# RMS norms of a two-layer decoder trunk: ScalarE takes the logarithm of the mean straight from PSUM, and VectorE makes the mean for Newton's step from the same PSUM tile

## The chip, the core and the metric

The kernel runs on one core of a Trainium2 chip. A core has five engines that each work through a program of their own, in order: TensorE (PE; its weight loads are shown as PEld), VectorE (DVE), ScalarE (ACT), GpSimd (POOL) and SyncE (SP), which here issues nearly all DMAs. They wait for one another through semaphores. The metric is device time in microseconds for one execution, as the median of several.

## What is computed

A decoder trunk of two layers over 1024 tokens of width 1024: an mLSTM layer with an MLP, a shared low-rank key/value latent, then a latent attention layer with an MLP. What matters here is the norm, which stands in front of and behind every block:

```python
def rmsnorm(x, g):
    xf = x.astype(jnp.float32)
    y = xf * lax.rsqrt(jnp.mean(xf * xf, axis=-1, keepdims=True) + EPS)
    return (y * g.astype(jnp.float32)).astype(x.dtype)

x = x + g1[:, None, :] * rmsnorm(y, norm_g[l, 1])
h = modulate(rmsnorm(x, norm_g[l, 2]), sh2, sc2)
y = sqrelu_mlp(h, mlp_w1[l], mlp_w2[l])
x = x + g2[:, None, :] * rmsnorm(y, norm_g[l, 3])
```

The latents of the attention layer (`c_kv`, 256 wide, and `cq`, 384 wide) are normed in the same way.

## The kernel before

**Layout.** Activations are held transposed: features on the 128 partitions, tokens along the free dimension, in two halves of 512 tokens. A tensor of width 1024 is eight tiles of 128x512. Each projection is done in three matrix products on values split into a high and a low part (L280, L281, L282). VectorE and ScalarE split the weights (`wsplit`: ScalarE L238 copies the high part, VectorE L239 subtracts) and the activations (`split_mod`: ScalarE L499, VectorE L500), and they empty PSUM.

**The norm.** `square_to` squares the tiles on ScalarE (L482) and adds them on VectorE (L486). `sums_rstd` (L488) multiplies the sum with a matrix of ones on TensorE (L490), so that every partition of a PSUM tile `pc` (128x512) holds the sum over the features of each token. VectorE reads that tile and makes the mean plus epsilon, `v` (L492). `rsqrt_` then takes the logarithm of `v` on ScalarE (L455), the exponential of minus half of it (L456), which is a first value `y` of the reciprocal root, and improves it on VectorE by a step of Newton's method in three instructions (L457, L458, L459): square of `y`, times `v` times -0.5, plus 1.5 times `y`. `sums_rstd` runs 16 times in the program, each time on 128x512. `rsqrt_` is also called 18 times on 128x4 tiles from other places (L535, L861 feed it), which the change leaves as they are.

**Who uses it.** `residual` (L939) multiplies the output of a block by the result (L950) and adds the old stream to it (L953); for the second attention half the old stream comes back by DMA into `tmc` tiles (`x_cols`, L920), and the new one goes out by DMA (L956). `post` and `post_second` norm the new stream and multiply it (L509). `latent` norms the key/value latent and the query latent (`cq`: L1690, applied on VectorE at L1706 and split by L499 and L500).

**What runs beside it.** The dense MLP of one token half runs beside the mixer of the other (`two_streams`). In it `hid` adds two PSUM tiles into kept ones: L1083 and L1084 read one `ps` tile, of which there are two, and `squares` (L980, L981 on ScalarE) squares the result. L1209 and L1211 load weights and copy them.

**What sets the order.** The program is recorded in Python in one order. The tile framework then schedules it with its own timing simulation, so each engine's order is its outcome, with `high_priority` and `issue_after` as hints. After that each engine keeps its order strictly. The framework also adds the waits: after a writer, before a buffer is reused, and between engines that read the same PSUM tile. The `tmc` tiles come from a ring of six, the `pc` and `ps` tiles from two each.

Of the kernel before, what the change touches and what calls it, by code (L numbers as in the profile page):

```python
# [9 lines left out]
F32 = mybir.dt.float32  # L10
# [3 lines left out]
AF = mybir.ActivationFunctionType  # L14
# [3 lines left out]
P = 128  # L18
# [6 lines left out]
EPS = 1e-6  # L25
# [57 lines left out]
def kernel(  # L83
# [27 lines left out]
    nc = tc.nc  # L111
# [26 lines left out]
    def tmc(dt=F32):  # L138
        return sb.tile([P, 512], dt, tag="tmc", bufs=TMC, name=f"tmc_{next(uid)}")
# [10 lines left out]
    def pc():  # L150
        return pp.tile([P, 512], F32, tag="pc", bufs=2, name=f"pc_{next(uid)}")
# [7 lines left out]
    def const(shape, dt, name):  # L159
        return sb.tile(shape, dt, tag=name, bufs=1, name=name)  # L160
# [287 lines left out]
    mcol = const([NH, 9], F32, "mcol")  # L448
    nc.vector.memset(mcol, 0.0)
    Cst = const([P, 4, VE], F32, "Cst")  # L450


    def rsqrt_(y, v, t):

        nc.scalar.activation(t, v, AF.Ln)  # L455
        nc.scalar.activation(y, t, AF.Exp, scale=-0.5)  # L456
        nc.vector.tensor_mul(t, y, y)  # L457
        nc.vector.scalar_tensor_tensor(t, t, -0.5, v, ALU.mult, ALU.mult)  # L458
        nc.vector.scalar_tensor_tensor(y, t, 1.5, y, ALU.add, ALU.mult)  # L459
# [12 lines left out]
    def rstd_steps(blocks, n):  # L472

        accs = []
        for b in blocks:
            square_to(accs, b)
        yield
        return sums_rstd(accs[0], n, tmc())
# [9 lines left out]
    def sums_rstd(acc, n, y):  # L488
        pt = pc()
        nc.tensor.matmul(pt, ones, acc, start=True, stop=True)  # L490
        v, t = tmc(), acc
        nc.vector.tensor_scalar(v, pt, 1.0 / n, EPS, ALU.mult, ALU.add)  # L492
        rsqrt_(y, v, t)
        return y

    def split_mod(hi, lo, u, sh):
# [37 lines left out]
    def rms_rows(v):  # L534
        nc.vector.tensor_scalar(v, v, 1.0 / D, EPS, ALU.mult, ALU.add)  # L535
        y, w = small(4), small(4)
        rsqrt_(y, v, w)
        return y
# [271 lines left out]
    def chunks0(hf):  # L810
# [4 lines left out]
        for j in range(4):  # L815
# [31 lines left out]
            for q, nv in enumerate(nvs):  # L847

                d, y, ss = small(4), small(4), small(4)
                sq = tmc()  # L850
                nc.scalar.activation(
                    sq.rearrange("p (b i e) -> p b i e", b=2, i=2), nv[:, :, :, 0:128], AF.Square
                )
                den = nv[:, :, :, 128]
                nc.vector.tensor_scalar(m4(y), den, -1.0, None, ALU.mult)
                nc.vector.tensor_max(m4(d), den, m4(y))
                enm = hf.gc[:, j, 16 + 4 * q : 20 + 4 * q].rearrange("p (i b) -> p b i", b=2)
                nc.vector.tensor_max(m4(d), m4(d), enm)
                nc.vector.scalar_tensor_tensor(d, d, EPS, d, ALU.mult, ALU.mult)
                nc.vector.reduce_sum(ss, sq.rearrange("p (a e) -> p a e", e=P), axis=AX.X)  # L860
                nc.vector.scalar_tensor_tensor(d, ss, 1.0 / P, d, ALU.mult, ALU.add)  # L861
                rsqrt_(y, d, ss)
                t1 = tmc()
                nc.vector.tensor_mul(
                    t1.rearrange("p (b i e) -> p b i e", b=2, i=2), nv[:, :, :, 0:128],
                    m4(y).unsqueeze(3).to_broadcast([P, 2, 2, P]),
                )
                t1s.append(t1)
# [736 lines left out]
    def latent(hf, behind):  # L1605
# [47 lines left out]
        def scaled(o, m):  # L1653

            pt = proj(m)
            if m < 2:

                evac(o, pt)
                pt = o

            if not rx:
                rx.append(sums_rstd(hf.xx, D, Cst.rearrange("p a b -> p (a b)")[:, :H]))
            nc.vector.tensor_mul(o, pt, rx[0])
            return o
# [1273 lines left out]
```

## Time and profile before

| | us |
|---|---|
| median of 3 runs (lowest, highest) | 2321.11 (2319.03, 2321.47) |
| the profiled execution's own time | 2317.84 |
| its span, first to last instruction | 2316.1 |
| TensorE busy, weight loads busy | 2276.3, 1918.0 |
| VectorE, ScalarE, GpSimd busy | 1698.5, 1126.6, 84.1 |
| mean granted TensorE clock | 0.997 |

A profile shows one execution. "Busy" counts time in which an engine had an instruction running; matrix products overlap, so a busy TensorE may still be slowed. A list of waits gives, for each engine and line, how long it stood idle and which engine's instruction released it. A timeline prints each instruction's start, duration, engine, line, operation and tiles, and in brackets the idle time before it and who ended it.

### The profile page before, as it was taken

Reading aid. Unit: us, or ns where it says so; the run is one execution under the profiler, and the core shown is the slowest. Engines: PE = TensorE matmul, PEld = TensorE weight load, DVE = VectorE, ACT = ScalarE, POOL = GpSimd, SP = SyncE. Lnnn points to the kernel's source line nnn. Section 1 sums busy time; section 2 is a strip of 40 time slices with the busy share of each in tenths; the row PEclk is TensorE's granted clock in tenths of the full one; section 3 lists DMA queues with packets and bytes.
Section 4 is the critical chain, followed back from the end, with each engine's and each line's share of the span. In section 5 each row is a group of like instructions: output and inputs, shape, how many; then the busy total and the mean of one; then the engine's idle time right before and its main releaser. Section 6 shows DMA issues by size and latency. Waiting matters only on the chain.

```text
span 2316.1 us, 32512 instructions
## 1 busy us (share of the span) xinstructions
PE 2276.3 (98%) x12010; PEld 1918.0 (83%) x12010; DVE 1698.5 (73%) x2782; ACT 1126.6 (49%) x1919; POOL 84.1 (4%) x164
## 2 busy tenths in 40 slices
PE   8999999999999999999999999999999999999998
PEld 6888788888887878778888788888888888989997
DVE  6676777889887877777765687666666388788776
ACT  4365435765334445545444555433444354555453
POOL 1000000001122210000000000000000000000000
PEclk9999999999999999999999999999999999999999
DMA  9543464668999887656775654764324352445432
GB/s 314 180 129 112 135 182 154 196 221 266 329 282 295 284 293 259 195 187 204 242 253 192 225 197 151 254 230 157 129 95 157 107 168 82 153 144 176 125 110 110
DMA packets 401647, 444.36 MB, mean 192 GB/s; under 512 B 27123, under 2 KB 289328, under 8 KB 401488
## 3 DMA queue, kind: packets, MB, share of 16 engines
q1 hardware_dynamic: 388544, 397.09, 53.6%
q0 software_dynamic: 12944, 45.20, 5.3%
q8 instruction: 94, 1.54, 0.3%
q14 instruction: 65, 0.53, 0.1%
HBM read 343.65 MB, written 98.57 MB: 191 GB/s over the span
## 4 chain that ended last, share of the span: by engine, by line
PE 75%; DMA 9%; DVE 9%; issue 4%; ACT 2%; POOL 0%; SPq 0%; DVEq 0%; ACTq 0%; POOLq 0%
PE ps L280 13%; PE ps L282 13%; PE ps L281 13%; PE pm L280 8%; PE pm L281 8%; PE pm L282 8%; DMA raw<-in_mlp_w_dram 4%; PE pc L281 2%; PE pc L280 2%; PE pc L282 2%; DMA raw<-s 1%; DVE wl L239 1%; DVE k L247 1%; PE pc L1988 1%; DVE sm L1791 1%
## 5 line engine op out<-in xcount | busy, mean ns | idle before, releaser
L238 ACT CAST wh<-raw 128x1024 fp32r<-128x1024 f32 (+2 forms) x317 | 321.4, 1016 | 437.2 <-PE ps L281 177.4
L239 DVE TENSOR_TENSOR wl<-raw,wh 128x1024 fp32r<-128x1024 f32 (+2 forms) x317 | 375.3, 1186 | 202.6 <-ACT wh L238 169.9
L280 PE MATMUL ps<-k,wh 128*128 128x512 f32 (+1 forms) x1252 | 476.0, 380 | 4.8 <-DVE tmc L1084 1.4
L282 PE MATMUL ps<-k,wl 128*128 128x512 f32 (+1 forms) x1252 | 468.4, 374 | 0.5 <-DVE wl L239 0.5
L281 PE MATMUL ps<-k,wh 128*128 128x512 f32 (+1 forms) x1252 | 467.9, 374 | 0.0
L280 PEld LDWEIGHTS ps<-k,wh 128*128 128x128 f32 x1252 | 236.2, 189 | 51.9 <-issue 2.8
L282 PEld LDWEIGHTS ps<-k,wl 128*128 128x128 f32 x1252 | 236.0, 189 | 43.4 <-DVE wl L239 1.0
L281 PEld LDWEIGHTS ps<-k,wh 128*128 128x128 f32 x1252 | 236.3, 189 | 41.4 <-issue 1.4
L247 DVE TENSOR_TENSOR k<-k,pm 128x512 f32<-128x512 f32 (+1 forms) x250 | 192.5, 801 | 63.3 <-PE pm L282 62.8
L280 PE MATMUL pm<-wh,hd 128*128 128x512 f32 x488 | 193.5, 396 | 3.5 <-ACT raw L1793 2.3
L282 PE MATMUL pm<-wh,hd 128*128 128x512 f32 x488 | 190.5, 390 | 0.0
L281 PE MATMUL pm<-wl,hd 128*128 128x512 f32 x488 | 190.3, 390 | 0.0
L280 PEld LDWEIGHTS pm<-wh,hd 128*128 128x128 f32 x488 | 91.7, 188 | 25.3 <-ACT raw L1793 4.6
L282 PEld LDWEIGHTS pm<-wh,hd 128*128 128x128 f32 x488 | 91.6, 188 | 19.9 <-DVE hd L500 0.5
L281 PEld LDWEIGHTS pm<-wl,hd 128*128 128x128 f32 x488 | 91.8, 188 | 18.4 <-issue 0.5
L390 DVE SCALAR_TENSOR_TENSOR tma<-raw,cond,tma 128x512 f32<-128x512 f32 x120 | 89.6, 747 | 16.6 <-DMA raw<-in_ada_w_dram 7.8
L281 PE MATMUL pm<-hd,wk 128*128 128x512 f32 x256 | 100.0, 391 | 1.7 <-DVE hd L500 1.7
L1793 ACT ACTIVATE raw<-pm,sm 128x128 f32<-128x128 f32 (+3 forms) x64 | 47.6, 743 | 111.0 <-DVE sm L1792 106.4
L280 PE MATMUL pm<-hd,wk 128*128 128x512 f32 x256 | 100.9, 394 | 0.6 <-ACT hd L499 0.6
L280 PE MATMUL pm<-hd,wh 128*128 128x512 f32 x256 | 99.2, 389 | 1.1 <-ACT hd L499 1.1
L282 PE MATMUL pm<-hd,wl 128*128 128x512 f32 x256 | 99.8, 390 | 0.1
L281 PE MATMUL pm<-hd,wh 128*128 128x512 f32 x256 | 99.6, 390 | 0.2 <-DVE hd L500 0.2
(497 smaller groups left out, 4828.1 us busy)
## 6 DMA issues: line engine op xcount, KB each, us to landing
raw<-in_mlp_w_dram SPq DMA_DIRECT2D x176, 512.0 KB, 4.5
raw<-in_ada_w_dram SPq DMA_DIRECT2D x64, 512.0 KB, 4.6
raw<-in_mlp_w_dram SPq DMA_DIRECT2D x128, 256.0 KB, 4.7
raw<-in_a_w_in_dram SPq DMA_DIRECT2D x44, 512.0 KB, 4.5
lo<-wl POOLq DMA_DIRECT2D x32, 512.0 KB, 6.1
wk<-lo SPq DMA_DIRECT2D x64, 256.0 KB, 4.4
xs<-k SPq DMA_DIRECT2D x40, 256.0 KB, 4.7
raw<-in_a_w_out_dram SPq DMA_DIRECT2D x16, 512.0 KB, 4.9
```

Source lines behind the costliest of these rows:

```text
L238: nc.scalar.copy(hi[:, :n], r[:, :n])
L239: i = nc.vector.tensor_sub(lo[:, :n], r[:, :n], hi[:, :n].bitcast(F32))
L247: return f(*a, **k)
L280: nc.tensor.matmul(o, lh, rh, start=start, stop=False)
L281: nc.tensor.matmul(o, lh, rl, start=False, stop=False)
L282: pe_last[0] = nc.tensor.matmul(o, ll, rh, start=False, stop=stop)
L390: nc.vector.scalar_tensor_tensor(acc, r[kk], cond[:, k : k + 1], acc, ALU.mult, ALU.add)
L1791: nc.vector.reduce_max(m, f, axis=AX.X, negate=True)
L1793: nc.scalar.activation(pr[:, :n], f, AF.Exp, bias=m, scale=SCALE, accum_out=l)
L1988: nc.tensor.transpose(pt[:, ts(m, P)], u.prs[i][:, ts(kb, P)], ident)
```

## The change

`sums_rstd` no longer calls `rsqrt_`. ScalarE takes the logarithm straight from the PSUM tile, with the scale 1/n as an immediate and epsilon from a new constant tile `epsc` as the bias; the exponential follows; VectorE then makes the mean `v` from the same PSUM tile, and `newton` holds the three instructions that stood at the end of `rsqrt_`. The other callers of `rsqrt_` execute what they did.

```diff
+    epsc = const([P, 1], F32, "epsc")
+    nc.vector.memset(epsc, EPS)
 
     def rsqrt_(y, v, t):
 
         nc.scalar.activation(t, v, AF.Ln)
         nc.scalar.activation(y, t, AF.Exp, scale=-0.5)
+        newton(y, v, t)
+
+    def newton(y, v, t):
+
         nc.vector.tensor_mul(t, y, y)
         nc.vector.scalar_tensor_tensor(t, t, -0.5, v, ALU.mult, ALU.mult)
         nc.vector.scalar_tensor_tensor(y, t, 1.5, y, ALU.add, ALU.mult)
...
         pt = pc()
         nc.tensor.matmul(pt, ones, acc, start=True, stop=True)
         v, t = tmc(), acc
+        nc.scalar.activation(t, pt, AF.Ln, bias=epsc, scale=1.0 / n)
+        nc.scalar.activation(y, t, AF.Exp, scale=-0.5)
         nc.vector.tensor_scalar(v, pt, 1.0 / n, EPS, ALU.mult, ALU.add)
-        rsqrt_(y, v, t)
+        newton(y, v, t)
         return y
```

In the changed program later lines have moved down: the logarithm is L498, the exponential L499, the mean L500, Newton's step L463 to L465, and lines from there on are 6 to 8 higher than before. The numbers behind tile names are 2 higher.

The scheduler moves other instructions around the 16 norms. Three places matter for the prediction.

The first is the norm of the query latent of the first half (`cq`), on VectorE. `pc_8823` (now `pc_8825`) is the PSUM tile of the sum, `ps_8895` (now `ps_8897`) a PSUM tile of the MLP, and L1706 (now L1714) applies the norm. In brackets is what the instruction waits for. Before:

```order
L457 TENSOR_TENSOR tmc_8723<-tmc_8822 128x512 [waits Activation_49]
L458 SCALAR_TENSOR_TENSOR tmc_8723<-tmc_8723,tmc_8825 128x512 [waits DVE_49]
L459 SCALAR_TENSOR_TENSOR tmc_8822<-tmc_8723,tmc_8822 128x512 [waits DVE_49]
L1083 TENSOR_TENSOR tmp_8741<-tmp_8741,ps_8895 128x512 [waits PE_49]
L1084 TENSOR_TENSOR tmc_8740<-tmc_8740,ps_8895 128x512 [waits DMAHW4_49]
L1706 SCALAR_TENSOR_TENSOR k_1470_8501<-k_1470_8501,cols,tmc_8822 128x512 [waits DVE_49]
L1706 SCALAR_TENSOR_TENSOR k_1470_8501<-k_1470_8501,cols,tmc_8822 128x512
L1706 SCALAR_TENSOR_TENSOR k_1471_8502<-k_1471_8502,cols,tmc_8822 128x512
```

And in the changed program, from the mean on:

```order
L500 TENSOR_SCALAR tmc_8827<-pc_8825 128x512 [waits Activation_49]
L463 TENSOR_TENSOR tmc_8725<-tmc_8824 128x512 [waits Activation_49]
L508 TENSOR_TENSOR hd_8819<-u_1462_8463,hd_8819 128x512 [waits Activation_49]
L464 SCALAR_TENSOR_TENSOR tmc_8725<-tmc_8725,tmc_8827 128x512 [waits DVE_49]
L465 SCALAR_TENSOR_TENSOR tmc_8824<-tmc_8725,tmc_8824 128x512 [waits DVE_49]
L1714 SCALAR_TENSOR_TENSOR k_1470_8503<-k_1470_8503,cols,tmc_8824 128x512 [waits DVE_49]
L1714 SCALAR_TENSOR_TENSOR k_1470_8503<-k_1470_8503,cols,tmc_8824 128x512
L1714 SCALAR_TENSOR_TENSOR k_1471_8504<-k_1471_8504,cols,tmc_8824 128x512
L1091 TENSOR_TENSOR tmp_8743<-tmp_8743,ps_8897 128x512 [waits PE_49]
L1092 TENSOR_TENSOR tmc_8742<-tmc_8742,ps_8897 128x512 [waits DMAHW4_49]
```

The three instructions that apply the norm have moved ahead of the two that empty the MLP's PSUM tile, and the mean, which waited for TensorE, now waits for ScalarE.

The second is ScalarE at the same norm. `u_1462` belongs to the MLP. Before:

```order
L980 ACTIVATE u_1462_8461<-u_1462_8461 128x512 [waits DVE_49]
L981 ACTIVATE u_1462_8461<-u_1462_8461 128x512 [waits Activation_49]
L455 ACTIVATE tmc_8723<-tmc_8825 128x512 [waits DVE_49]
L499 CAST hd_8817<-u_1462_8461 128x512 [waits Activation_49]
L456 ACTIVATE tmc_8822<-tmc_8723 128x512 [waits Activation_49]
```

And in the changed program:

```order
L988 ACTIVATE u_1462_8463<-u_1462_8463 128x512 [waits DVE_49]
L498 ACTIVATE tmc_8725<-pc_8825,epsc 128x512 [waits PE_49]
L989 ACTIVATE u_1462_8463<-u_1462_8463 128x512 [waits Activation_49]
L499 ACTIVATE tmc_8824<-tmc_8725 128x512 [waits Activation_49]
L507 CAST hd_8819<-u_1462_8463 128x512 [waits Activation_49]
```

The logarithm has moved up by one place and the exponential ahead of the MLP's copy; one instruction of the MLP stands between the two, as before.

The third is SP's queue behind the norm of the first attention half's residual. `tmc_11883` and `tmc_11888` (now `tmc_11885` and `tmc_11890`) are tiles of the old stream, `wk`, `raw` are MLP weights. Before:

```order
L920 DMA tmc_11878<-xs 128x512
L1210 DMA wk_11930<-lo_3886 128x512 x2
L1209 DMA raw_12079<-in_mlp_w_dram 128x2x256 x2
L1073 DMA raw_12113<-s_3884 128x1024
L956 DMA xs<-k_2012_11287 128x512
L956 DMA xs<-k_2013_11288 128x512 x2
L920 DMA tmc_11883<-xs 128x512
L920 DMA tmc_11888<-xs 128x512
```

And in the changed program:

```order
L928 DMA tmc_11880<-xs 128x512
L964 DMA xs<-k_2012_11289 128x512
L928 DMA tmc_11885<-xs 128x512
L1218 DMA wk_11932<-lo_3888 128x512 x2
L1217 DMA raw_12081<-in_mlp_w_dram 128x2x256 x2
L1081 DMA raw_12115<-s_3886 128x1024
L964 DMA xs<-k_2013_11290 128x512 x2
L928 DMA tmc_11890<-xs 128x512
```

One store and one load of the old stream have moved ahead of three loads of weights.

## The prediction

> **What bounds the kernel now.** I read the page's busy times and chain first, then the list of waits, then the norm's own lines, and last the timelines of the places where TensorE stops near a norm.
>
> ```profile
> span 2316.1 us, 32512 instructions
> PE 2276.3 (98%) x12010; PEld 1918.0 (83%) x12010; DVE 1698.5 (73%) x2782; ACT 1126.6 (49%) x1919; POOL 84.1 (4%) x164
> PE 75%; DMA 9%; DVE 9%; issue 4%; ACT 2%; POOL 0%; SPq 0%; DVEq 0%; ACTq 0%; POOLq 0%
> ```
>
> TensorE is busy for 2276.3 of 2316.1 us and makes three quarters of the chain. The change gives TensorE no less to do, so it can win only part of the 39.8 us in which TensorE stands, and much of that lies in the start, far from any norm. VectorE and ScalarE have room on average; what counts is what they finish late.
>
> The norm's own lines, from the view of each source line (minimum/median/maximum ns, first and last start):
>
> ```profile
> L492 DVE TENSOR_SCALAR tmc<-pc x16: 681/688/692, 403.5 to 1897.4; 128x512 f32<-128x512 f32 x16
> L455 ACT ACTIVATE tmc<-tmc x16: 613/632/636, 404.2 to 1898.1; 128x512 f32<-128x512 f32 x16
> L457 DVE TENSOR_TENSOR tmc<-tmc x14: 681/691/693, 407.1 to 1899.4; 128x512 f32<-128x512 f32 x14
> ```
>
> Mean, logarithm, exponential, then three instructions of Newton's step, all in a row: 0.69 + 2 x 0.63 + 3 x 0.69, some 4.0 us, and 16 of these. If every one lay on TensorE's path and the mean's 0.69 us fell out, the kernel would win 16 x 0.7 = 11 us. Does TensorE wait for them? I took twenty microseconds from each of the 16 sums on, in one view by windows; here is its sum and two of its rows:
>
> ```profile
> 950.00:970.00 20.00, 18.39 (x89) 14.53 (x88) 16.20 (x26) 14.28 (x24) 0.00 (x0) 1.00 0.62 187
> 1315.00:1335.00 20.00, 18.66 (x81) 14.76 (x80) 16.90 (x26) 15.34 (x24) 0.39 (x4) 1.00 0.56 178
> sum 320.00, PE 316.99 PEld 255.74 DVE 263.76 ACT 197.67 POOL 4.17; mean PE 19.81 PEld 15.98 DVE 16.48 ACT 12.35 POOL 0.26
> ```
>
> The columns are the window, its length, then PE, PEld, DVE, ACT and POOL busy. TensorE stands for 3.0 us in all 16 windows, 1.6 of it in the window at 950 and 1.3 in that at 1315. Behind the other 14 norms it works through the other token half meanwhile, and a norm that is ready 0.7 us sooner moves nothing. So the gain is cut from 11 us to what three places can give: the two windows, and the stretch at 1285 to 1291 that follows from the norm at 1258.
>
> **The change, part by part.** *Not side by side.* Both engines now read the same PSUM tile. The order shows the mean waiting for ScalarE instead of TensorE, and the kernel before has the same pattern in L570 (ScalarE) and L572 (VectorE), which read one PSUM tile and share nothing else:
>
> ```profile
> L572 DVE SCALAR_TENSOR_TENSOR tmc<-ps,mods,tmp x8: 741/750/753, 149.2 to 195.1; 128x512 f32<-128x512 f32 x8
>   ACT tmp L570: 4.6, 6
> ```
>
> VectorE stood 4.6 us in six of eight cases until ScalarE had read. So the mean will run beside the exponential, not beside the logarithm: the path from the sum is logarithm, then the longer of mean and exponential (0.69 against 0.63), then Newton's step, and 0.63 + 0.03 us fall out of it where both engines are free. The Trainium skill ("PSUM — Partial Sum Buffer", section "PSUM bank collisions raise a hardware error") says more: two engines must not even read one bank of the same partitions at once, since readers then get wrong data, so it has to be guarded by bank. By that rule the order here is a must, and the rival of true side-by-side work, below, would be out; by the row alone it is only what the framework does.
>
> *The price of it.* VectorE works in order. The mean used to be issued as soon as TensorE was done; now it, and all behind it, also waits until ScalarE has come to the logarithm. Where ScalarE is busy, the gain is gone. The norm of `cq` at 951 shows this (VectorE, ScalarE and TensorE in their timelines):
>
> ```profile
> 951.26 1.02 PE L490 MATMUL pc<-tmc,ones 128*128 128x512 f32 x2
> 952.18 0.63 ACT L980 ACTIVATE u<-u 128x512 f32<-128x512 f32 x1
> 952.53 0.68 DVE L492 TENSOR_SCALAR tmc<-pc 128x512 f32<-128x512 f32 x1
> 952.84 0.63 ACT L981 ACTIVATE u<-u 128x512 f32<-128x512 f32 x1
> 954.41 0.63 ACT L456 ACTIVATE tmc<-tmc 128x512 f32<-128x512 f32 x1
> 955.15 0.69 DVE L457 TENSOR_TENSOR tmc<-tmc 128x512 f32<-128x512 f32 x1
> 956.59 0.69 DVE L459 SCALAR_TENSOR_TENSOR tmc<-tmc,tmc 128x512 f32<-128x512 f32 x1
> 957.51 0.39 PE L282 MATMUL ps<-k,wl 128*128 128x512 f32 x1
> 957.93 0.69 DVE L1083 TENSOR_TENSOR tmp<-tmp,ps 128x512 f32<-128x512 f32 x1 [0.65 <-PE ps L282]
> 958.54 0.68 DVE L1084 TENSOR_TENSOR tmc<-tmc,ps 128x512 f32<-128x512 f32 x1
> 959.13 2.07 DVE L1706 SCALAR_TENSOR_TENSOR k<-k,cols,tmc 128x512 f32<-128x512 f32 x3
> 959.27 0.50 PE L280 MATMUL ps<-k,wh 128*128 128x512 f32 x1 [1.38 <-DVE tmc L1084]
> 964.26 0.50 PE L281 MATMUL pc<-k,wh 128*128 128x512 f32 x1 [0.24 <-DVE k L500]
> ```
>
> After the change: ScalarE ends L980 at 952.8, the logarithm at 953.5, L981 at 954.1, the exponential at 954.7 (0.63 each, starts 0.66 apart or less). The mean runs from 953.5 to 954.2, a microsecond later than now; the square starts at 954.8, and the MLP's L500 now comes between it and the rest, so Newton's step ends at about 957.4, against 956.59 + 0.69 = 957.28 now. Nothing is won. But the scheduler has put the three L1706 ahead of L1083 and L1084. They run from 957.4 to 959.4, and L1083 and L1084, now done by 959.22, end at 960.6. TensorE, which has had nothing to write into since 957.9, starts at 960.65 instead of 959.27: its wait grows from 1.38 to 2.75, **1.35 us lost**. The split of `cq` follows sooner, so the 0.24 at 964.26 goes away: **+1.1 us** net. Bounds: +0.4, if the norm ends 0.7 sooner than I say; +4.1, if the clock drops too (below).
>
> *The norm at 1258* (residual of the first attention half). TensorE does not stop there, but from 1285 on it does, and a late load is behind it:
>
> ```profile
> 1274.79 1.83 SPq L920 DMA_DIRECT2D tmc<-xs  x2
> 1282.52 1.36 DVE L953 TENSOR_TENSOR k<-k,tmc 128x512 f32<-128x512 f32 x2 [1.67 <-DMA tmc<-xs]
> 1285.13 0.50 PE L280 MATMUL ps<-k,wh 128*128 128x512 f32 x1 [0.79 <-DVE u L247]
> 1290.09 0.50 PE L280 MATMUL pm<-hd,wk 128*128 128x512 f32 x1 [0.58 <-ACT hd L499]
> 1290.93 0.50 PE L281 MATMUL pm<-hd,wk 128*128 128x512 f32 x1 [0.34 <-DVE hd L500]
> ```
>
> The last two tiles of the old stream are asked for at 1274.79, and VectorE, blocked at L953 until 1282.52, is late with L247. In the new queue one of the two is asked for ahead of three weight loads, some 4 us sooner, and only one L953 is left behind the wait. L247 then comes one instruction (0.69) sooner, and most of 0.79 + 0.58 + 0.34 = 1.71 goes: I take **-1.0 us**, with bounds -1.7 (all of it) and +0.8 (the earlier load lands late all the same, VectorE stands at it ahead of L1083, and the weights behind it are late).
>
> *The norm at 1316.*
>
> ```profile
> 1320.18 0.69 DVE L500 TENSOR_TENSOR hd<-u,hd 128x512 fp32r<-128x512 f32 x1 [1.41 <-ACT hd L499]
> 1328.83 0.50 PE L281 MATMUL pm<-hd,wk 128*128 128x512 f32 x1 [1.34 <-DVE hd L500]
> ```
>
> VectorE stands 1.41 us until 1320.18, then runs nearly without a gap into the L500 that TensorE waits for. The changed order puts the square first, which needs the exponential, and that stands behind L980, the logarithm and L981; it can start at about 1320.35. The same instructions follow: **+0.2 us**, bounds -0.7 and +0.7 (one instruction either way).
>
> *The rest.* The other 13 norms: 0, covered by TensorE's work on the other half; without that cover each would be worth up to 0.7, and I allow +-1 for all. The constant's memset is one instruction of 128x1 in the start: 0. The logarithm's bias comes from a tile, its source from PSUM; neither takes it far from 0.63. Sum: 1.1 - 1.0 + 0.2 = **+0.3 us** on the profiled execution (2316.1 of span and 1.7 around it, 2317.84). The median stands 3.27 above that execution, so I add the term to the median: 2321.11 + 0.3, rounded **2321.4 us**, no change.
>
> **The rivals.** *Slower: the wait at 959 lets the clock drop.* After the longest stop in the program the granted clock (the figure behind the busy times) fell:
>
> ```profile
> 1014.78 0.77 PE L280 MATMUL pc<-k,wh 128*128 128x512 f32 x1 [3.73 <-DVE hd L500]
> 1015.00:1021.00 6.00, 6.00 (x15) 4.71 (x16) 3.83 (x11) 1.78 (x4) 0.00 (x0) 0.53 0.58 173
> 1021.00:1027.00 6.00, 6.00 (x30) 4.95 (x29) 1.73 (x3) 2.84 (x4) 0.00 (x0) 1.00 0.67 218
> ```
>
> At a clock of 0.53 TensorE started 15 products in 6 us, then 30: the stop cost 3.0 us on top of its 3.73. After 1.38 us the clock holds, so the point from which it decides lies between 1.38 and 3.73, and 2.75 is inside. Then the place at 951 costs 4.1, and if the load at 1274 gives nothing as well, the sum is 4.1 + 0.2 + 0.5 of the rest: 2325.9. For it: the order of L1706 is certain. Against it: 2.75 is a microsecond short of the only stop that did this. The Trainium skill ("TensorE: Matmul & The Clock Gate", section "Why this matters for your kernels") warns of idle gaps over about 3 us; by that rule 2.75 would just be spared.
>
> *Faster: the stop at 1014 shortens.* It ends on a load that ScalarE waits for, and all before it shifts by about a microsecond. If the stop falls under the point from which the clock drops, 3.0 us go, with a microsecond or so of the stop; with -1.7 at 1285 and +1.3 elsewhere that is 2321.11 - 4.7 = 2316.4. Against it: from 965 on the order of VectorE, ScalarE and TensorE is unchanged there, and the loads are paced by TensorE, so a delay shifts both.
>
> *The change does what it says*, mean beside logarithm: then L1706 at 951 starts 0.7 sooner, that term is +0.4 and the sum -0.4 (2320.7), still no change. The waits in the order speak against it.
>
> **How the numbers follow.** Forecast 0.53, slower by the clock or by several small stops in the new order 0.24, faster 0.18, side by side 0.05. The second and third go over 0.2% either way (4.6 us, about what a measurement of this kernel tells from no change): slower 0.24, faster 0.18, and same 0.53 + 0.05 = 0.58. The range takes in both ends: 2316.4 below, 2325.9 above, and about a microsecond for the spread of the runs: 2315.5 to 2327.0. The likeliest case alone has -1.7 + 0.4 - 0.7 to 1.1 + 0.8 + 0.7, so 2319 to 2324.
>
> **What would show it.** The mean's row should name ScalarE's logarithm as what it waits for, and start within 0.1 us of its end. The wait of L280 for L1092 (L1084 before) should read about 2.7, and the clock after it tell between forecast and first rival. The stops at 1285 and 1290 should be mostly gone, that at 1328 be there still, and the windows behind the other norms stay full. I am wrong if TensorE's standing time near the norms changes by more than 3 us, if a stop appears behind one of the 13 quiet norms (a later mean holding back a weight split, L239), or if the total moves though these places don't.

## The result and the profile after

| | before | changed |
|---|---|---|
| median of the runs shown with the result, us | 2319.49 (2318.23 to 2321.47, 6 runs) | 2333.72 (2331.88 to 2336.37, 6 runs) |
| ratio, 95% interval | | 1.0065 [1.0054, 1.0076] |
| profiled execution: its time, its span, us | 2317.84, 2316.1 | 2333.1, 2331.3 |

The changed kernel is 14.2 us slower than the kernel before; 2321.4 us, 0.3 more than before, had been forecast, and the result lies above the range. The page of the changed kernel, its span, its busy times and its chain by engine:

```profile
span 2331.3 us, 32526 instructions
PE 2294.7 (98%) x12010; PEld 1915.0 (82%) x12010; DVE 1699.0 (73%) x2783; ACT 1126.3 (48%) x1919; POOL 84.1 (4%) x164
PE 84%; DVE 6%; DMA 5%; issue 2%; ACT 2%; SPq 0%; POOL 0%; DVEq 0%; ACTq 0%; POOLq 0%
```

The three lines answer to those of before, and they rule out what I had looked for as the cause of the 14 us. TensorE stands **less** than before: 2331.3 - 2294.7 = 36.6 us against 39.8. It is its busy time that grew, 18.4 us for the same 12010 products, and 18.4 - 3.2 = 15.2 is the whole difference of the two spans. VectorE and ScalarE are as busy as they were. So the waits did not grow in sum (one at 951 did, by 1.2 us, as shown below); the products themselves became slower.

Which ones? The view of source lines with shapes kept apart, its columns being engine, operation, tiles and shape, count, then busy sum, mean ns of one, and idle time ahead. A product's mean here runs from start to modelled end and overlaps its neighbours; since these rows follow each other in turn, a difference of the means is a difference in their pace. In `ps<-k,wl` the first input, `k`, moves through TensorE, and the second, `wl`, is loaded as weights. Before:

```profile
L280 PE MATMUL ps<-k,wh 128*128 128x512 f32 x1060 | 421.5, 398 | 4.8 <-DVE tmc L1084 1.4 <-DVE sm L1792 1.0 <-ACT wh L238 0.9
L282 PE MATMUL ps<-k,wl 128*128 128x512 f32 x1060 | 414.1, 391 | 0.5 <-DVE wl L239 0.5
L281 PE MATMUL ps<-k,wh 128*128 128x512 f32 x1060 | 413.5, 390 | 0.0
L282 PE MATMUL pm<-wh,hd 128*128 128x512 f32 x488 | 190.5, 390 | 0.0
L281 PE MATMUL ps<-wl,k 128*128 128x256 f32 x224 | 63.4, 283 | 0.0
```

and after the change:

```profile
L280 PE MATMUL ps<-k,wh 128*128 128x512 f32 x1060 | 427.4, 403 | 4.8 <-DVE tmc L1092 2.6 <-ACT wh L238 1.3 <-DVE sm L1800 0.8
L282 PE MATMUL ps<-k,wl 128*128 128x512 f32 x1060 | 420.6, 397 | 0.7 <-DVE wl L239 0.7
L281 PE MATMUL ps<-k,wh 128*128 128x512 f32 x1060 | 420.4, 397 | 0.0
L282 PE MATMUL pm<-wh,hd 128*128 128x512 f32 x488 | 190.5, 390 | 0.0
L281 PE MATMUL ps<-wl,k 128*128 128x256 f32 x224 | 62.6, 280 | 0.0
```

The products of 512 columns that move a `k4` tile against split weights take about 6 ns more in these large groups; those that move split weights against `hd` take what they took; those of 256 columns are 3 ns faster in the row shown. A window far from any norm, in which TensorE never stands, has the loss too, in plain count. Before, then after (window, length, then PE with its starts, PEld, DVE, ACT, POOL, granted clock, DMA share, GB/s):

```profile
640.00:700.00 60.00, 60.00 (x272) 49.62 (x270) 51.40 (x78) 24.77 (x41) 14.67 (x20) 1.00 0.95 291
```

```profile
640.00:700.00 60.00, 60.00 (x266) 48.86 (x265) 52.38 (x79) 22.13 (x37) 13.91 (x18) 1.00 0.93 284
```

272 products in 60 us, then 266, at a granted clock of 1.00 in both: 2.2% fewer, and it isn't the clock.

What differs for `k4` and not for `hd`? The change allocates one new tile, `epsc`, 128x1, right behind `Cst`. In the program's table the allocator gives a tile whole multiples of 32 bytes of each partition, in the order of first use. From that table (first byte in a partition; large tiles lie 4096 apart):

```
              before              changed
cols          41664               41664
k4   first    42656               42656
Cst           144352              144352
epsc          -                   146432
ws   first    147104              147136   (wh, wl, wv, lw, wk)
hd   first    179872              179904
tmc  first    212640              212672
```

`k4` was claimed ahead of the new tile and stays; split weights (tag `ws`), `hd` and `tmc` move up by 32 bytes. Before, the distance from `k4` to the weights is 104448, a multiple of 2048; now it is 32 more. Between weights and `hd` it is 32768 in both.

### The profile page after: what moved, and what is told of

Read it like the earlier page. It is cut to its first block, busy times and chain, and to the rows that moved or that the text cites. A ratio compares the mean times of both kernels' runs of the same rounds, so it can differ in the third digit from the quotient of the medians.

```text
span 2331.3 us, 32526 instructions
## 1 busy us (share of the span) xinstructions
PE 2294.7 (98%) x12010; PEld 1915.0 (82%) x12010; DVE 1699.0 (73%) x2783; ACT 1126.3 (48%) x1919; POOL 84.1 (4%) x164
## 4 chain that ended last, share of the span: by engine, by line
PE 84%; DVE 6%; DMA 5%; issue 2%; ACT 2%; SPq 0%; POOL 0%; DVEq 0%; ACTq 0%; POOLq 0%
PE ps L280 14%; PE ps L282 14%; PE ps L281 14%; PE pm L280 9%; PE pm L281 9%; PE pm L282 9%; DMA raw<-in_mlp_w_dram 2%; PE pc L280 2%; PE pc L281 2%; PE pc L282 2%; DVE wl L239 1%; PE pc L1996 1%; DVE k L247 1%; PE pm L841 1%; DVE sm L1799 1%
## 5 line engine op out<-in xcount | busy, mean ns | idle before, releaser
L280 PE MATMUL ps<-k,wh 128*128 128x512 f32 (+1 forms) x1252 | 481.7, 385 | 4.8 <-DVE tmc L1092 2.6
L282 PE MATMUL ps<-k,wl 128*128 128x512 f32 (+1 forms) x1252 | 474.6, 379 | 0.7 <-DVE wl L239 0.7
L281 PE MATMUL ps<-k,wh 128*128 128x512 f32 (+1 forms) x1252 | 474.3, 379 | 0.0
L280 PEld LDWEIGHTS ps<-k,wh 128*128 128x128 f32 x1252 | 236.3, 189 | 56.4 <-DVE tmc L1092 3.0
L282 PEld LDWEIGHTS ps<-k,wl 128*128 128x128 f32 x1252 | 236.0, 189 | 49.7 <-DVE wl L239 1.6
L281 PEld LDWEIGHTS ps<-k,wh 128*128 128x128 f32 x1252 | 236.3, 189 | 46.3 <-issue 1.2
L280 PE MATMUL pm<-wh,hd 128*128 128x512 f32 x488 | 193.5, 397 | 3.1 <-ACT raw L1801 2.8
L282 PE MATMUL pm<-wh,hd 128*128 128x512 f32 x488 | 190.5, 390 | 0.0
L281 PE MATMUL pm<-wl,hd 128*128 128x512 f32 x488 | 190.4, 390 | 0.0
L280 PEld LDWEIGHTS pm<-wh,hd 128*128 128x128 f32 x488 | 91.6, 188 | 24.8 <-ACT raw L1801 5.1
L282 PEld LDWEIGHTS pm<-wh,hd 128*128 128x128 f32 x488 | 91.6, 188 | 20.0 <-DVE hd L508 0.4
L281 PEld LDWEIGHTS pm<-wl,hd 128*128 128x128 f32 x488 | 91.7, 188 | 18.5 <-issue 0.5
L281 PE MATMUL pm<-hd,wk 128*128 128x512 f32 x256 | 100.1, 391 | 1.8 <-DVE hd L508 1.8
L280 PE MATMUL pm<-hd,wk 128*128 128x512 f32 x256 | 100.9, 394 | 0.0
L281 PE MATMUL pm<-hd,wh 128*128 128x512 f32 x256 | 100.1, 392 | 0.2 <-DVE hd L508 0.2
L280 PE MATMUL pm<-hd,wh 128*128 128x512 f32 x256 | 99.3, 390 | 0.7 <-ACT hd L507 0.7
L282 PE MATMUL pm<-hd,wk 128*128 128x512 f32 x256 | 99.8, 390 | 0.0
```

What stands on the lines that cost most here:

```text
L280: nc.tensor.matmul(o, lh, rh, start=start, stop=False)
L281: nc.tensor.matmul(o, lh, rl, start=False, stop=False)
L282: pe_last[0] = nc.tensor.matmul(o, ll, rh, start=False, stop=stop)
```

## The experiments

Theory A: a product's time depends on the distance between its moving operand and its weights in the partition. Theory B: the new order of instructions around the norms makes the 14 us. Theory C: weights (or `k4`) at certain places are slow by themselves. Where a tile was only added, the order on all five engines is that of its parent, instruction by instruction, so that addresses alone differ. The results together, with the distances modulo 256 (medians in us; the kernel before had 2319.36 to 2320.66 in the runs that these were compared with, and the ratios are against those):

| kernel | k4 to weights | weights to hd | median | ratio, 95% interval |
|---|---|---|---|---|
| changed | 32 | 0 | 2333.72 | 1.0065 [1.0054, 1.0076] |
| before, one column behind `Cst` | 32 | 0 | 2334.6 | 1.0064 [1.0051, 1.0076] |
| changed, one column more | 64 | 0 | 2333.21 | 1.0062 [1.0050, 1.0074] |
| before, `k4` +32, weights +64 | 32 | 0 | 2334.29 | 1.0064 [1.0052, 1.0076] |
| before, `hd` and `tmc` +32 | 0 | 32 | 2332.53 | 1.0059 [1.0047, 1.0072] |
| before, all +32 | 0 | 0 | 2321.57 | 1.0004 [0.9995, 1.0013] |
| changed, all +32 | 0 | 0 | 2320.09 | 0.9994 [0.9984, 1.0004] |
| changed, weights +128 | 128 | 0 | 2338.78 | 1.0081 [1.0065, 1.0096] |
| changed, weights +192 | 192 | 0 | 2321.91 | 1.0011 [1.0002, 1.0020] |
| changed, weights +256 | 0 | 0 | 2319.96 | 0.9999 [0.9991, 1.0008] |
| changed, all +32, norm of cq as before | 0 | 0 | 2320.28 | 1.0003 [0.9994, 1.0012] |

**The kernel before, with the place alone changed.**

```diff
     Cst = const([P, 4, VE], F32, "Cst")
+    const([P, 1], F32, "pad")
```

> The kernel before, with one unused column of 128x1 allocated behind Cst, where the change put its constant. Norms, operations and their order on every engine are those of the kernel before; only the tiles allocated later (weight splits, hd, tmc) lie 32 bytes higher, and k4, allocated earlier, stays. Theory A (addresses: a product of 512 columns is slower when its moving tile and its weights start 32 bytes apart modulo 64): the 4050 products of k4 with split weights go from 227 to about 233 ns, +22 us, those of 256 columns win about 4, so 2334 to 2340 us. Theory B (the new order of the norms makes the 14 us): no change, 2319.5 within 1.5.

2334.6 us: the whole loss, without a norm touched and without a new instruction. Theory B falls here. The same row as above:

```profile
L281 PE MATMUL ps<-k,wh 128*128 128x512 f32 x1060 | 420.4, 397 | 0.0
```

**The changed kernel, 64 bytes instead of 32.**

```diff
     epsc = const([P, 1], F32, "epsc")
+    const([P, 1], F32, "pad")
```

> The changed kernel with a second unused column of 128x1 behind its constant, so that weight splits, hd and tmc lie 64 bytes higher than before and stand to k4 as before modulo 64; norms and order are those of the changed kernel. Theory A: the 22 us on products of k4 with split weights go away and the norm's own effect is left: 2314 to 2321 us. Theory B: 2333.7 within 1.5, as the changed kernel. If 64 bytes are as bad as 32: also 2333 or more, but then with products at 233 ns, and the run of the kernel before with one column must be slow too.

2333.21 us: no better. That was a miss for theory A as I had it: 64 bytes are as bad as 32 (mean 396 for the row above), so the modulus is not 64. By itself this run would have spoken for B; the first one had excluded that.

**Both moved, but not by the same.** The column ahead of the column table moves `k4` too:

```diff
+    const([P, 1], F32, "pad")
     cols = const([P, 200 + 48], F32, "cols")
...
     Cst = const([P, 4, VE], F32, "Cst")
+    const([P, 1], F32, "pad2")
```

> The kernel before with one unused column ahead of the column table and one behind Cst: k4 lies 32 bytes higher (at 0 modulo 64), weight splits and hd 64 higher (at 32 modulo 64). Order unchanged. Theory A (the distance counts): slow again, 2334 to 2340 us, k4 with split weights at 233 ns. Theory C (weights that start at 0 modulo 64 are what is slow, wherever k4 lies): no change, 2319.5 within 1.5. Theory B: no change.

2334.29 us. The weights start at 32 modulo 64 as in the kernel before, and the kernel is slow all the same; theory C, in the form that weights at 0 modulo 64 are slow, falls.

**The other pair of tiles.**

```diff
+    const([P, 1], F32, "pad")
     p2 = Piece(4, 4, hd)
```

> The kernel before with one unused column allocated just ahead of the first hd tile: k4 and weight splits stay, hd and tmc lie 32 bytes higher. Order unchanged. Theory A: now the 1510 products that move hd against split weights and the 1473 that move split weights against hd get some 5.5 ns each, +16 us, and k4 with split weights stays at 227: 2332 to 2338 us. Theory C: no change, the weights have not moved. A rival of A, that k4 alone is sensitive: no change, 2319.5 within 1.5.

2332.53 us, and the loss has changed sides. Its rows:

```profile
L281 PE MATMUL ps<-k,wh 128*128 128x512 f32 x1060 | 413.4, 390 | 0.0
L282 PE MATMUL pm<-wh,hd 128*128 128x512 f32 x488 | 193.0, 396 | 0.0
```

`k4` against weights is at 390 again; weights moved against `hd` went from 390 to 396. Neither the place of `k4` nor that of the weights has changed here, and it is also not the moving tile's kind, since here the split weights move and `hd` is what is loaded. What the four have in common is the distance.

**The distance by itself.** A kernel of products only, one source line for each series of 100, of which one execution was taken (`w` and `m` are the series' offsets in columns of 4 bytes):

```
for k in range(100): nc.tensor.matmul(o[:, :512], wt[:, w + k % 4 * 128 : w + 128 + k % 4 * 128], mv[:, m:m+512], ...)
```

> Nothing of the model is computed: 22 series of 100 products alone on TensorE, one source line each, from one moving tile and one tile of weights (four weights of 512 bytes in turn), no other engine busy, the output zeros. The first 16 series and the last have 512 columns, five with weights 0, 32, 64, 128, 256 bytes off and one with both tiles 32 off have 256. Theory A2 (a product of 512 columns runs at 227 ns only where the distance of moving operand and weights is 0 modulo some power of two above 64; 32 and 64 were both slow): distance 0 gives 22.7 us a series, 32, 64 and 96 give 23.3, and the first of 128 and 256 that gives 22.7 again is the modulus. If the weights' own place counted (theory C), moving the moving operand by 32 or 64 would change nothing, and moving both would be slow. Rival D (TensorE loses the time only while VectorE, ScalarE or transfers read the same memory): all series alike. For 256 columns A2 has the opposite sign from the traces: 12.0 us at distance 0, 11.7 at 32 and 64.

The view of source lines (the busy sum of 100 products is their pace, plus about 0.2 us of the last one's end). Lines 123 to 130 have the weights 0, 32, 64, 96, 128, 160, 192 and 224 bytes off (125 and 128, left out, read 23.5), 131 has 256, 133 and 134 have the moving operand 32 and 64 off, 135 both 32, 137 the weights 16; 138 and 140 are 256 columns at 0 and 64:

```profile
L126 PE MATMUL o<-mv,wt 128*128 128x512 f32 x100 | 23.6, 396 | 0.0
L137 PE MATMUL o<-mv,wt 128*128 128x512 f32 x100 | 23.5, 396 | 0.0
...
L133 PE MATMUL o<-mv,wt 128*128 128x512 f32 x100 | 23.5, 395 | 0.0
L124 PE MATMUL o<-mv,wt 128*128 128x512 f32 x100 | 23.5, 395 | 0.0
L130 PE MATMUL o<-mv,wt 128*128 128x512 f32 x100 | 23.5, 395 | 0.0
...
L127 PE MATMUL o<-mv,wt 128*128 128x512 f32 x100 | 23.4, 394 | 0.0
...
L134 PE MATMUL o<-mv,wt 128*128 128x512 f32 x100 | 23.1, 391 | 0.0
L129 PE MATMUL o<-mv,wt 128*128 128x512 f32 x100 | 23.1, 391 | 0.0
L135 PE MATMUL o<-mv,wt 128*128 128x512 f32 x100 | 22.9, 389 | 0.0
...
L123 PE MATMUL o<-mv,wt 128*128 128x512 f32 x100 | 22.8, 389 | 0.0
L131 PE MATMUL o<-mv,wt 128*128 128x512 f32 x100 | 22.8, 389 | 0.0
...
L138 PE MATMUL o<-mv,wt 128*128 128x256 f32 x100 | 12.2, 283 | 0.0
...
L140 PE MATMUL o<-mv,wt 128*128 128x256 f32 x100 | 11.9, 281 | 0.0
```

Only 0 and 256 give 22.8 us; 16 to 160 and 224 give 23.4 to 23.6; 192 lies between. Both operands moved together: 22.9. So the distance counts, and a multiple of 256 bytes is what is good. Beside these series VectorE and ScalarE do nothing and the transfers next to nothing (a DMA share of 0.00 in the first 60 us), so the loss is TensorE's own (the rival in which another engine disturbs it falls). The starts of this trace give 226.7 ns a product at 0, 233.3 at 32 and 64, 232.4 at 128 and 229.0 at 192. They also show that the difference counts with its sign: the moving operand 64 off, a distance of -64 or 192 modulo 256, takes 229.0 like weights at 192, and 32 off takes 233.3 like weights at 224. With 256 columns the sign of the effect turns, as in the kernel: 119.9 at 0, 117.8 at 64.

**All tiles moved together, with the old norms and with the new.**

```diff
+    const([P, 1], F32, "pad")
     cols = const([P, 200 + 48], F32, "cols")
```

> The kernel before with one unused column of 128x1 ahead of the column table: k4, weight splits, hd and tmc all lie 32 bytes higher, their distances stay, order unchanged. Theory A2: no change, 2319.4 within 2, k4 with split weights at 227 ns. Theory C (absolute places): weights now start at 0 modulo 64, as in the slow runs, so 2332 to 2337.

2321.57 us, no change: weights at 0 modulo 64 and `k4` at 0 modulo 64 harm nothing so long as they move together. In the changed kernel the constant itself goes there:

```diff
+    epsc = const([P, 1], F32, "epsc")
+    nc.vector.memset(epsc, EPS)
     cols = const([P, 200 + 48], F32, "cols")
...
-    epsc = const([P, 1], F32, "epsc")
-    nc.vector.memset(epsc, EPS)
```

> The changed kernel with its constant allocated and set ahead of the column table, not behind Cst: norms as changed, all large tiles shifted by the same 32 bytes, order that of the changed kernel but for the memset. Theory A2: the loss is gone, 2316 to 2321 us, with the norms' own effect, which the changed kernel against the kernel before with one column puts at 2333.7 - 2334.6 = -0.9 us, so 2318.5. Theory B (order of the norms): 2333.7. The stop at TensorE's L280 behind L1092 stays at 2.6 us.

2320.09 us, ratio 0.9994 [0.9984, 1.0004]: the loss is gone with the new norms in place. What is left for the new norms is -0.0006 of 2320, that is -1.4 us, between -3.7 and +0.9.

**The modulus in the whole kernel.** Behind `epsc` in the changed kernel stands one more unused tile, of 96, 160 or 224 bytes:

```diff
     epsc = const([P, 1], F32, "epsc")
+    const([P, 24], F32, "pad")
```

> The changed kernel with 96 unused bytes (128x24) behind its constant: weight splits, hd and tmc lie 128 bytes higher than before against k4. If the distance counts modulo 128: as the changed kernel with its constant early, 2316 to 2321 us, and the series at 128 bytes at 22.7 us. If modulo 256 or 512: 2332 to 2336, and that series at 23.3.

> The same with 160 unused bytes (128x40), distance 192. The series at 192 took 229.0 ns a product against 226.7 at 0 and 233.3 at 32. Theory A2 forecasts the part of the loss by that figure: 4050 products by 2.3 ns is 9 us, less about 3 for those of 256 columns: 2326, between 2323 and 2329. A theory of good and bad distances without steps between: 2320 or 2333 to 2338.

> The changed kernel with 224 unused bytes (128x56) behind its constant: weight splits, hd and tmc lie 256 bytes higher against k4 than before. Theory A2 with modulus 256 (from the series): k4 with split weights at 227 ns, 2320 within 2, as the changed kernel with its constant early. If only a multiple of 512 or the unshifted place were good in the whole kernel: 2332 or more.

128 bytes have the highest median of all, 2338.78 us, above what I had expected: the products of 512 columns are slow (the row of L281 at 395), and those of 256 win less than at 32, 282 against 280 in their row. 256 bytes are as good as none, 2319.96. At 192 I had expected 2326 from the series and it was 2321.91; the rows show why:

```profile
L280 PE MATMUL ps<-k,wh 128*128 128x512 f32 x1060 | 423.6, 400 | 7.6 <-DVE tmc L1093 2.6 <-DVE sm L1801 1.4 <-ACT wh L238 1.4
L282 PE MATMUL ps<-k,wl 128*128 128x512 f32 x1060 | 416.1, 393 | 0.5 <-DVE wl L239 0.5
L281 PE MATMUL ps<-k,wh 128*128 128x512 f32 x1060 | 414.1, 391 | 0.0
```

By the busy sums L280 and L282 lose 2.0 ns a product there (423.6 against 421.5 and 416.1 against 414.1, over 1060), near the 2.3 of the series, but L281 only 0.6 (414.1 against 413.5). That makes 1.5 on average, while the 256-column products keep the whole gain that they have at 32 (62.6 in the row of L281 `ps<-wl,k`, as there, against 63.4 before). The series uses four neighbouring weights in turn, the kernel weights from several tiles; which part of that matters wasn't tried.

**The term at 951 by itself.** In the changed kernel with its constant early, the norm of `cq` alone (n = 384) goes back to the old way:

```diff
         v, t = tmc(), acc
+        if n == 384:
+            nc.vector.tensor_scalar(v, pt, 1.0 / n, EPS, ALU.mult, ALU.add)
+            rsqrt_(y, v, t)
+            return y
         nc.scalar.activation(t, pt, AF.Ln, bias=epsc, scale=1.0 / n)
```

> The changed kernel with its constant early, and the norm of cq alone (n = 384) taken back to the old way, in which VectorE's mean goes first. That puts L1092 ahead of two of the three instructions that scale cq again. If the term at 951 was right: TensorE's stop at L280 behind L1092 goes from 2.55 back to about 1.4, the clock does not drop behind it, and some 1.2 + 1.3 us go, 2317.5 against 2320.1, about what can be measured. If the stop stays, the order of VectorE was not its cause.

TensorE's timeline at the place:

```profile
960.84 0.50 PE L280 MATMUL ps<-k,wh 128*128 128x512 f32 x1 [1.38 <-DVE tmc L1096]
```

The stop is back at 1.38 from the 2.55 of the changed kernel with its constant early, and VectorE's L1095 and L1096 again run ahead of L1718 (L1714 in the changed kernel). So the new norm of `cq`, with the order that it brings, is its cause. In the time nothing of it shows: 2320.28 against 2320.09, where 2317.5 was expected. 1.2 us of a stop, and about as much of the slower clock that followed it in the trace with the constant early, are at the edge of what these runs can tell (an interval of some 2 us either way), so this term is shown in the trace alone.

**Finer distances and other widths.**

> Again nothing of the model, only series of products with one source line each. Weights 4, 8, 224, 240, 248, 252 and 512 bytes off: 512 as 0 (22.7 us for 100), the small ones tell whether the loss comes at once (233 ns) or in steps. A series of pairs on two lines, weights at 0 and then at 32: if a product's time is set by the weights that are loaded while it streams (the next product's), the line with weights at 0 is the slow one; if by its own weights, the line with 32; either way 23.0 us per 100 together. Then 384, 320, 448, 272 and 128 columns at 0 and 32: 448 and 384 should lose at 32 as 512 does, 272 and 320 tell where the sign turns, 128 should be set by the loading of weights, alike at both.

Again one execution. Lines 124 to 130 have weights 4, 8, 224, 240, 248, 252 and 512 bytes off, 132 and 133 are the pair at 0 and 32 in turn, 139 and 140 are 448 columns at 0 and 32, 135 is 384 at 0, and 136, at 32, has the same 17.5:

```profile
L133 PE MATMUL o<-mv,wt 128*128 128x512 f32 x100 | 39.9, 399 | 0.0
L132 PE MATMUL o<-mv,wt 128*128 128x512 f32 x100 | 39.6, 396 | 0.0
...
L124 PE MATMUL o<-mv,wt 128*128 128x512 f32 x100 | 23.4, 394 | 0.0
...
L130 PE MATMUL o<-mv,wt 128*128 128x512 f32 x100 | 22.9, 389 | 0.0
...
L129 PE MATMUL o<-mv,wt 128*128 128x512 f32 x100 | 22.8, 389 | 0.0
L140 PE MATMUL o<-mv,wt 128*128 128x448 f32 x100 | 20.6, 366 | 0.0
L139 PE MATMUL o<-mv,wt 128*128 128x448 f32 x100 | 20.4, 365 | 0.0
L135 PE MATMUL o<-mv,wt 128*128 128x384 f32 x100 | 17.5, 334 | 0.0
```

4 bytes (L124) cost nearly all of it already, 4 bytes the other way (L129, 252) nothing, and there is no even slope: the starts give 232.4 ns at 4, 230.7 at 8, 228.4 at 240 and 233.4 at 248. 448 columns lose 0.2 us in 100, where 512 lose 0.6 or more; 384, against my expectation, nothing. The pair didn't decide between a product's own weights and the next one's: both lines are slow, 396 and 399 (235.0 ns a product by their starts), so mixing a good and a bad distance is no better than bad alone. Why the distance matters inside TensorE stays open.

## Why the prediction was wrong, point by point

*The step that failed* stands in its part on the rest: "The constant's memset is one instruction of 128x1 in the start: 0." The instruction does cost nothing. The tile that it fills costs the 14 us: 32 bytes between `k4` and all that is allocated later, which takes the distance of moving operand and weights off a multiple of 256. In the busy sums of the three largest rows alone this is 427.4 - 421.5 = 5.9 (L280), 6.5 (L282) and 6.9 (L281), together 19.3 us; the 256-column products give a few back, and in these two profiles TensorE, being slower, waits 3.2 us less for the others. I looked at what the change does in time, engine by engine, and not at what it does in memory, though the table of tiles was there to compare. None of the rivals had it either: all three were about waits.

*The norms themselves.* With the distances as before, the new norms come to 2319.96 (ratio 0.9999 [0.9991, 1.0008], so -0.2 us, between -2.1 and +1.9) and 2320.09. The forecast of +0.3 for them agrees with that, as far as some 2 us either way can tell. The argument that 14 of the 16 norms lie behind TensorE's work was right. The view by windows of twenty microseconds from each of the 16 sums on, taken of the changed kernel, has this sum:

```profile
sum 320.00, PE 316.10 PEld 251.46 DVE 271.35 ACT 195.68 POOL 4.71; mean PE 19.76 PEld 15.72 DVE 16.96 ACT 12.23 POOL 0.29
```

TensorE stands 3.9 us in them instead of 3.0, 2.57 in the window at 960 and 1.33 in that at 1328, and not at all in the other 14.

*Not side by side: right.* The mean's and the logarithm's own lines in the changed kernel, and the norm of `cq` in the timeline:

```profile
L500 DVE TENSOR_SCALAR tmc<-pc x16: 682/690/692, 406.3 to 1915.1; 128x512 f32<-128x512 f32 x16
...
  ACT tmc L498: 17.4, 8
...
L498 ACT ACTIVATE tmc<-pc,epsc x16: 669/688/690, 404.7 to 1913.8; 128x512 f32<-128x512 f32 x16
```

```profile
961.48 0.67 ACT L498 ACTIVATE tmc<-pc,epsc 128x512 f32<-128x512 f32 x1
962.19 0.69 DVE L500 TENSOR_SCALAR tmc<-pc 128x512 f32<-128x512 f32 x1 [0.20 <-ACT tmc L498]
965.88 2.08 DVE L1714 SCALAR_TENSOR_TENSOR k<-k,cols,tmc 128x512 f32<-128x512 f32 x3
...
968.48 0.68 DVE L1092 TENSOR_TENSOR tmc<-tmc,ps 128x512 f32<-128x512 f32 x1
969.21 0.80 PE L280 MATMUL ps<-k,wh 128*128 128x512 f32 x1 [2.57 <-DVE tmc L1092]
```

VectorE stood 17.4 us in eight of the 16 means until ScalarE had read, and here the mean starts 0.04 us behind the logarithm's end (961.48 + 0.67). The rival of side-by-side work is out. The logarithm from PSUM with the bias tile took 0.69 in the median, where "neither takes it far from 0.63" had been said: 0.06 too short in each of the 16, and rows of before had the price. There ScalarE's instructions of this shape took 0.63 from SBUF without a bias tile (L981, mean 631 ns), 0.72 with one (L502, 717), 0.59 from PSUM without one (L1307, 592) and 0.69 from PSUM with one (L1793, 688, which also adds up its outputs). The rule of the Trainium skill ("PSUM — Partial Sum Buffer", section "PSUM bank collisions raise a hardware error"), by which two engines must not read one bank together, fits this order; what would happen without it no run here shows.

*The terms of the sum.* At 951 the three L1714 come first and the stop is 2.57, where I had worked out 2.75; the stop of 0.24 at 964 is gone, as forecast. The clock is a case by itself (last section). At 1285 and 1290 the stops of 0.79, 0.58 and 0.34 have become one of 0.44, a gain of 1.27 where -1.0 was taken; at 1316 the stop stayed at 1.33 against 1.34, where +0.2 was taken:

```profile
1302.66 0.50 PE L281 MATMUL pm<-hd,wk 128*128 128x512 f32 x1 [0.44 <-DVE hd L508]
```

```profile
1340.83 0.50 PE L281 MATMUL pm<-hd,wk 128*128 128x512 f32 x1 [1.33 <-DVE hd L508]
```

Together that is (2.57 - 1.38 - 0.24) - 1.27 - 0.01 = 0.95 - 1.28, some -0.3 us instead of +0.3, plus about 1.4 in an execution in which the clock falls.

*The rivals.* "Slower" was given 0.24 for the clock behind 959. Its condition was met in the profiled execution, in which the clock fell behind the stop of 2.57, but that is worth about 1.4 us; the rest of the loss has another cause that this rival doesn't contain, so its 2325.9 isn't near either. "Faster": the stop at 1014 did not shorten, it is 4.05 in the changed kernel. (Its parts as written, 3.0, about 1, 1.7 and -1.3, add to 4.4 and not 4.7, which changes no conclusion.)

*What would make it wrong* had the right sentence last: "or if the total moves though these places don't". The places moved by about a microsecond each, much as forecast, and the total by 14; that is what sends a reader from the waits to the busy time.

## What to carry to other kernels

A new tile is a change of the memory map, however small: compare the addresses of moving operands and weights before and after, and keep their distance (here a multiple of 256 bytes for products of 512 columns), or allocate small constants ahead of both or behind both. When the busy time of the bounding engine grows at the same count and the same clock, look at the mean of single instructions, shape by shape, before looking for waits. A placebo, the old kernel with the new tile and nothing else, costs one run and would have told this change's two effects apart at once.

## What the runs showed of the hardware

*The distance of the two operands.* In the series a product of 128x512 took 226.7 ns with moving operand and weights at 0 or 256 bytes from each other and up to 234 at other distances; at 256 columns it is the good distance that is slower, 119.9 against 117.8. The Trainium skill ("SBUF — State Buffer", section "Who interferes with whom") gives TensorE two independent read ports, one for the moving operand and one for loading weights, and says that it never waits on anyone. If that also meant that the two ports never slow each other, all series would have been alike; they differ by 3% with VectorE and ScalarE idle, and the measurement decides.

*The clock behind a short stop.* I had taken it that 1.38 us of standing leave the clock alone and 3.73 drop it, with a point between that decides. The stop of 2.57 in the changed kernel was followed by 3 us at a clock of 0.50 with 7 products started; the same stop of 2.55 in the same program with weights 256 bytes on was not, with 13 started. First the window of the changed kernel, then stop and window of the other:

```profile
969.20:972.20 3.00, 2.99 (x7) 2.41 (x8) 3.00 (x6) 2.17 (x4) 0.00 (x0) 0.50 0.67 198
```

```profile
960.24 0.50 PE L280 MATMUL ps<-k,wh 128*128 128x512 f32 x1 [2.55 <-DVE tmc L1093]
```

```profile
960.20:963.20 3.00, 2.96 (x13) 2.47 (x14) 3.00 (x6) 2.33 (x5) 0.00 (x0) 1.00 0.69 207
```

Six kept traces have this stop of 2.53 to 2.57. In three of them the clock stood at 0.50 or 0.51 for the 3 us around or behind its end (changed, weights +128, constant early); in the other three it stayed at 1.00 (one column more, weights +192, weights +256). And in the kernel before with one column, a stop of 1.50 was followed by the half clock, 1.2 us after its end:

```profile
1005.06 0.44 PE L1916 MATMUL pc<-ident,raw 128*128 128x128 f32 x2 [1.50 <-DVE raw L1796]
```

```profile
1006.30:1009.30 3.00, 3.00 (x9) 2.11 (x9) 1.76 (x3) 2.08 (x4) 0.00 (x0) 0.51 0.00 0
```

So the length of the stop does not decide alone, in this range at least; what else does, no run here separates. The Trainium skill ("TensorE: Matmul & The Clock Gate", section "Why this matters for your kernels") asks for no gaps over about 3 us; here gaps of 1.50 and 2.57 were followed by the half clock. By the first two windows shown, such a stretch costs 13 - 7 = 6 products of 0.23, some 1.4 us by this estimate, a tenth of what the 32 bytes cost.
